# Last tile's products ahead of the first tiles' transposes, and one weights piece split by VectorE, in a two-layer decoder step

## The chip, the cores and the metric

The kernel runs on one core of a Trainium2 chip. The metric is the device time of one execution in microseconds. The core has five instruction streams: PE (TensorE: matrix products, transposes), DVE (VectorE), ACT (ScalarE), POOL (GpSimd) and SP, which here only issues transfers. Each runs its own instructions strictly in order and waits for the others on semaphores. An instruction that waits holds up everything behind it on its engine. Products land in PSUM, which has eight banks of 2 KB per partition; everything else lies in SBUF.

## The reference: what is computed

A two-layer decoder handles 512 prompt tokens and 8 x 4 = 32 sample tokens, 544 columns in all. Layer 0 mixes with a gated short convolution, layer 1 with multi-scale retention over four heads; each layer is followed by a SwiGLU feed-forward.

```python
x = x + mixer(rmsnorm(x))
x = x + (silu(h @ w_gate) * (h @ w_up)) @ w_down      # h = rmsnorm(x); 1024 -> 2816 -> 1024
```

Retention is computed in chunks. For each head and chunk it is

```python
scores = einsum(q, k) * decay
inner  = einsum(scores, v)
cross  = einsum(q, S) * cross_w
S_new  = S * chunk_decay + einsum(k * state_w, v)
```

and then `inner + cross` is normalised over the head's 512 columns (mean and variance), multiplied by `silu(g)` and a gain, and projected back. All is in float32.

## The kernel before

**Precision.** To keep float32 accuracy with the fast product type, each operand is split into a high half (rounded by ACT, `Copy` to fp32r) and a low half (the rest). Each product is then three: high by high, low by high, high by low. `split` (lines 182 to 184) lets ACT make the high half and DVE the low half by subtraction. `split_adding` (lines 186 to 190) spares DVE: ACT makes the high half and its negative, and a transfer issued by POOL adds the weights to that negative from memory. `load_piece` (line 131) loads one weights piece of 128 x 1024 by SP and takes the one or the other, by its argument `adding`. Weights buffers rotate through three slots.

**Feed-forward of a layer.** `whole_pairs` (line 524) does the first two rounds (m = 0 and 1) as plain products, four pieces each: gate for j = m and j = m + 11, then up for the same two (q = 0 and 1). Round 0's two gate pieces are interleaved by halves of k: first half of piece 0, first half of piece 1, second half of piece 0, second half of piece 1. All eight pieces of both layers come from `split_adding`. Ahead of that, the mixer's output projection adds its last tiles to x (L257), and `split_x` makes the halves of each tile of x (L194 on ACT, L195 on DVE), while POOL adds up squares (L210). The later rounds use a seven-product scheme with fewer products.

**Retention, per head.** After the values, gates and scores, the head works on four token tiles of 128 and on the sample rows:

- `inner(h, st, it)` (line 993) forms the products of one token tile into one PSUM bank: twelve for tiles 2 and 3.
- `sample_outputs(h, st, i)` (line 1046) multiplies the sample rows with the i-th quarter of the recurrent state S (four products, L1054, which the trace shows as eight), after S has been loaded by SP. S tiles rotate through three buffers, so the fourth (i = 3) is loaded once the first has been updated and written out.
- `states_update(h, st, i)` (line 1059) forms four products (L1070), adds them to the decayed S in two DVE steps (L1075) and writes S out (L1076).
- `normalized` (line 981) takes the statistics of a bank (L986, L987, L214 on DVE, the power -0.5 on POOL in L215) and writes the normalised tile to SBUF (L990). This frees the bank.
- `gated(h, st, yn, it)` (line 1010) transposes a normalised tile on PE (four transposes, L1014, into a bank) and multiplies the gate by it on DVE (L1017, or L1021 for the sample rows). This frees that bank.
- `qk_project(h + 1, ...)` (line 801) is the next head's key and query projection, 48 products of 272 columns each; given `inside`, it calls that between the two halves of k.

For heads 0 to 2 the next head's projections are interleaved with this head's last tiles (lines 1137 to 1158). Banks of this kind ("sm") are four: one collects the sample rows' outputs, the others are taken by tiles, transposes and the split projection, whichever is free in the order of the code. The order of instructions on each engine is then set by the framework's scheduler, by its own costs; `tc.issue_after` pins a start. In the order that was built before, the first two tiles' transposes have a bank each, and the last tile's products take the bank of the first.

Of the kernel before, what the change touches and what calls it, by code (L numbers as in the profile page):

```python
# [12 lines left out]
P = 128  # L13
D = 1024
KT = D // P
# [10 lines left out]
HJ = FJ // 2  # L26
# [19 lines left out]
def hybrid_decode_kernel(ctx: ExitStack, tc: tile.TileContext, a: dict, o: dict):  # L46
# [84 lines left out]
    def load_piece(src, n, parts=1, sw=None, keep=None, adding=False):  # L131

        if sw is None:
            w = wts.tile([P, n], F32, tag="w", name=nm("w"))
            wh, wl = parts2(n)
        else:
            w = sw.tile([P, n], F32, tag="w2", name=nm("w2"))
            wh, wl = parts2(n, sw, ("h2", "l2"))

        def load(i):  # L140
            c = slice(i * n // parts, (i + 1) * n // parts)
            last_load[0] = nc.sync.dma_start(w[:, c], src[:, c])
            if adding:
                split_adding(wh, wl, w, src)
            else:
                split(wh[:, c], wl[:, c], w[:, c])

        if keep is not None:
            keep.append(w)
        if parts > 1:  # L150
            return wh, wl, load
        load(0)
        return wh, wl
# [109 lines left out]
    with ExitStack() as c0:  # L263
# [7 lines left out]
        st = one.tile([P, KT, NB, 2], F32, tag="st", name="st")  # L271
# [221 lines left out]
    def ffn(layer, next_gain):  # L493
        with ExitStack() as c1:
            tp = c1.enter_context(tc.tile_pool(name=f"ff{layer}", bufs=4))
            fp = c1.enter_context(tc.tile_pool(name=f"ffp{layer}", bufs=2))
            sw = c1.enter_context(tc.tile_pool(name=f"sw{layer}", bufs=1))
# [26 lines left out]
            def whole_pairs():  # L524


                ks, us = list(range(KT)), []
                steps = rms_scale()
                for m in range(WHOLE):
                    gu, pts = [], []  # L530
                    ws = [
                        load_piece(a["ffgu"][layer, 2 * j + q], KT * P, sw=sw if m == 0 and q and j >= HJ else None, adding=True)
                        for q in range(2) for j in (m, m + HJ)
                    ]
                    for q in range(2):
                        pts.append([psum() for _ in range(2 - q)])
                        if m + q == 0:
                            for part in (ks[:KP], ks[KP:]):
                                for (wh, wl), pt in zip(ws, pts[0]):
                                    project(  # L540
                                        pt, wh, wl, 0, xh, xl, part[0] == ks[0], part[-1] == ks[-1], ks=part,
                                        weave=steps if part[0] else iter(()),
                                    )
                            continue
                        for i in range(2):
                            if i == len(pts[q]):
                                pts[q].append(psum())
                            project(pts[q][i], *ws[2 * q + i], 0, xh, xl, weave=steps)
                        drain(steps)
                    for q in range(2):  # L550
                        d = tp.tile([P, 2, T], F32, tag="gu", name=nm("gu"))
                        gu.append(d)
                        for i in range(2):
                            each(lambda p, di, r: nc.vector.tensor_mul(di, p, r), pts[q][i], halves(d[:, i, :]), R)
                            if q == 0:
                                nc.scalar.activation(d[:, i, :], d[:, i, :], AF.Silu)
                            else:
                                nc.vector.tensor_mul(d[:, i, :], d[:, i, :], gu[0][:, i, :])
                    us.append(gu[1])
                    for k in range(2 * m, KP if m == WHOLE - 1 else 2 * m + 2):  # L560
                        operand(k)
                return us
# [163 lines left out]
    with ExitStack() as c2:  # L726
# [74 lines left out]
        def qk_project(h, st, which, dt, inside=None):  # L801

            wh, wl = load_piece(a["rtqk"][h, which * 2 + dt], KT * P)
            pt = [bank(), bank()] if inside else psum()
            if inside:
                project(pt, wh, wl, 0, xh, xl, last=False, ks=range(KP))
                inside()
                project(pt, wh, wl, 0, xh, xl, first=False, ks=range(KP, KT))
            else:
                project(pt, wh, wl, 0, xh, xl)  # L810
            qk_rotate(st, which, dt, pt)
# [181 lines left out]
        def inner(h, st, it):  # L993

            vh, vl, _ = st["v"]
            qh, ql = st["q"]
            mh, ml = st["mid"]
            c = it // 2
            pt = bank()
            ts_ = token_tiles(it)  # L1000
            for dt in range(2 * c):
                mm3(pt, qh[:, dt, ts_], ql[:, dt, ts_], mh[:, dt, :], ml[:, dt, :], dt == 0, False)
            for jt in range(2 * c, it + 1):
                at = token_tiles((it % 2) if jt % 2 == 0 else 2)
                mm3(
                    pt, st["sh"][:, c, at], st["sl"][:, c, at], vh[:, jt, :], vl[:, jt, :], jt == 0, jt == it,
                )
            return pt
# [37 lines left out]
        def sample_outputs(h, st, i):  # L1046


            r, dt = RD[i]
            if i == 0:  # L1050
                st["po"] = bank()
                nc.tensor.matmul(st["po"], scp, st["vs"], start=True, stop=False, skip_group_check=True)
            for g in range(4):
                last_product[0] = nc.tensor.matmul(  # L1054
                    st["po"][32 * g : 32 * g + 8, :], qm[:, dt, g, r, :], st["S"][i][:, g, :],
                    start=False, stop=(i == 3), skip_group_check=True,
                )
# [51 lines left out]
        st = qk_start(0)  # L1109
        qk_first(st)  # L1110
        qk_project(0, st, 0, 1)
        for h in range(NH):
            more = h + 1 < NH
            value(h, st)
            st["S"] = {}
            for i in range(3):
                states_load(h, st, i)
            gate_project(h, st, 0)
            sample_operands(h, st)
            state(h, st, 0)  # L1120
            gate_project(h, st, 1)
            state(h, st, 1)
            for c in range(2):
                scores(h, st, c)
            if more:
                gate_project(h, st, 2)
                gate_project(h, st, 3)
            sample_outputs(h, st, 0)
            states_update(h, st, 0)
            states_load(h, st, 3)  # L1130
            yn0 = normalized(inner(h, st, 0))
            sample_outputs(h, st, 1)
            yn1 = normalized(inner(h, st, 1))
            states_update(h, st, 1)
            sample_outputs(h, st, 2)
            p2 = inner(h, st, 2)
            if more:
                nxt = qk_start(h + 1)
                for which in (1, 0):
                    qk_scale(nxt, which)  # L1140
                with tc.issue_after(last_product[0].ins):
                    qk_project(h + 1, nxt, 1, 0)
                with tc.issue_after(last_product[0].ins):
                    gated(h, st, yn0, 0)
                    gated(h, st, yn1, 1)
                yn2 = normalized(p2)
                sample_outputs(h, st, 3)
                p3 = inner(h, st, 3)
                yns = normalized(st["po"])
                states_update(h, st, 2)  # L1150
                gated(h, st, yn2, 2)
                yn3 = normalized(p3)
                qk_project(h + 1, nxt, 1, 1, lambda: states_update(h, st, 3))
                gated(h, st, yns, 4)
                gated(h, st, yn3, 3)
                qk_project(h + 1, nxt, 0, 0)
                qk_project(h + 1, nxt, 0, 1)
                out_project(h, st)
            else:
                yn2 = normalized(p2, "gt")  # L1160
                gate_project(h, st, 2, lambda: states_update(h, st, 2))
                sample_outputs(h, st, 3)
                yns = normalized(st["po"], "rot1")
                gate_project(h, st, 3, lambda: states_update(h, st, 3))
                for it, yn in enumerate((yn0, yn1, yn2)):
                    gated(h, st, yn, it)
                p3 = inner(h, st, 3)
                gated(h, st, yns, 4)
                yn3 = normalized(p3)
                out_project(h, st, [lambda: None, lambda: gated(h, st, yn3, 3)])  # L1170
            st = nxt
# [121 lines left out]
```

## Time and profile before

| | us |
|---|---|
| median of three runs | 1474.68 |
| lowest and highest | 1474.08, 1477.44 |
| the profiled execution | 1475.72 |
| its span | 1474.0 |
| PE busy | 1451.8 |
| DVE busy | 922.4 |
| ACT busy | 567.4 |
| POOL busy | 93.5 |

A row of the order of time gives the start and the length in microseconds from the span's start, the engine, the line of the kernel, the operation, "out <- in" by the program's names, the shape, and how many equal instructions it merges; in brackets stands how long the engine was idle before and what ended that. On PE, start to start is the better measure, since lengths overlap. A row of the list of waits gives the total, the number of times and the longest.

The last tiles of heads 0, 1 and 2, from the first tile's transposes to the next query projection, lie at 677.49 to 692.61, 804.10 to 818.76 and 930.23 to 944.88 us. Layer 1's feed-forward begins at 1084.27.

### The profile page before, as it was taken

Reading aid. Unit: us, or ns where it says so; the run is one execution under the profiler, and the core shown is the slowest. Engines: PE = TensorE matmul, PEld = TensorE weight load, DVE = VectorE, ACT = ScalarE, POOL = GpSimd, SP = SyncE. Lnnn points to the kernel's source line nnn. Section 1 sums busy time; section 2 is a strip of 40 time slices with the busy share of each in tenths; the row PEclk is TensorE's granted clock in tenths of the full one; section 3 lists DMA queues with packets and bytes.
Section 4 is the critical chain, followed back from the end, with each engine's and each line's share of the span. In section 5 each row is a group of like instructions: output and inputs, shape, how many; then the busy total and the mean of one; then the engine's idle time right before and its main releaser. Section 6 shows DMA issues by size and latency. Waiting matters only on the chain.

```text
span 1474.0 us, 25908 instructions
## 1 busy us (share of the span) xinstructions
PE 1451.8 (98%) x10954; PEld 1382.3 (94%) x10954; DVE 922.4 (63%) x1412; ACT 567.4 (38%) x805; POOL 93.5 (6%) x118
## 2 busy tenths in 40 slices
PE   8999999999999999999999999999999999999997
PEld 8999999999999999897987988888799999999996
DVE  5644439847748647648545834845849847748644
ACT  5222355625525434242142224214265625525333
POOL 2100220000000003000000000000030000000003
PEclk9999999999999999999999999999999999999998
DMA  5222264232322325336335613713474232322322
GB/s 210 87 93 94 89 169 108 96 103 88 103 95 87 101 65 190 106 115 233 98 115 171 201 58 117 267 34 139 172 171 116 92 106 90 94 94 91 98 66 81
DMA packets 69461, 173.36 MB, mean 118 GB/s; under 512 B 6480, under 2 KB 22992, under 8 KB 69344
## 3 DMA queue, kind: packets, MB, share of 16 engines
q1 hardware_dynamic: 66432, 162.12, 32.5%
q0 software_dynamic: 2336, 8.46, 3.4%
q8 instruction: 86, 1.41, 0.4%
q10 hardware_dynamic: 576, 1.11, 0.2%
q14 instruction: 31, 0.25, 0.1%
HBM read 150.50 MB, written 21.18 MB: 116 GB/s over the span
## 4 chain that ended last, share of the span: by engine, by line
PE 93%; DMA 4%; DVE 1%; ACT 1%; POOL 0%; issue 0%; SPq 0%; DVEq 0%; POOLq 0%; ACTq 0%
PE mm L170 41%; PE sm L427 26%; PE sm L170 14%; PE sm L848 2%; PE sm L849 2%; DMA S<-in_rets_dram 2%; PE sm L850 2%; PE sm L158 1%; PE sm L159 1%; PE sm L160 1%; DMA out_rets_dram<-S 1%; PE sm L1054 1%; PE mm L855 1%; DMA wl<-in_ffgu_dram 1%; DVE S L1075 0%; PE sm L1014 0%
## 5 line engine op out<-in xcount | busy, mean ns | idle before, releaser
L183 ACT ACTIVATE wh<-w 128x1024 fp32r<-128x1024 f32 (+2 forms) x211 | 208.4, 990 | 456.7 <-PE mm L170 271.8
L184 DVE TENSOR_TENSOR wl<-w,wh 128x1024 fp32r<-128x1024 f32 (+2 forms) x211 | 242.3, 1151 | 39.8 <-ACT wh L183 36.4
L170 PE MATMUL mm<-xh,wh 128*128 128x272 f32 x1060 | 221.7, 290 | 6.6 <-ACT wh L183 6.6
L170 PE MATMUL mm<-xh,wl 128*128 128x272 f32 x1060 | 219.6, 289 | 1.6 <-DMA wl<-in_ffgu_dram 1.6
L170 PE MATMUL mm<-xl,wh 128*128 128x272 f32 x1060 | 218.5, 288 | 0.0
L170 PEld LDWEIGHTS mm<-xh,wh 128*128 128x128 f32 x1060 | 166.4, 189 | 11.3 <-ACT wh L183 6.6
L170 PEld LDWEIGHTS mm<-xh,wl 128*128 128x128 f32 x1060 | 165.6, 189 | 2.2 <-DMA wl<-in_ffgu_dram 1.8
L427 PE MATMUL sm<-oh,wh 128*128 128x272 f32 x576 | 166.5, 289 | 0.0
L427 PE MATMUL sm<-oh,wl 128*128 128x272 f32 x576 | 166.5, 289 | 0.0
L170 PEld LDWEIGHTS mm<-xl,wh 128*128 128x128 f32 x1060 | 166.3, 189 | 0.0
L427 PE MATMUL sm<-ol,wh 128*128 128x272 f32 x576 | 166.2, 289 | 0.0
L257 DVE TENSOR_TENSOR x<-x,mm 128x544 f32<-128x544 f32 x85 | 61.2, 720 | 146.4 <-PE mm L170 146.4
L427 PE MATMUL sm<-oh,l 128*128 128x272 f32 x432 | 124.8, 289 | 0.0
L427 PE MATMUL sm<-ol,h 128*128 128x272 f32 x432 | 124.7, 289 | 0.0
L427 PE MATMUL sm<-oh,h 128*128 128x272 f32 x432 | 124.7, 289 | 0.0
L427 PEld LDWEIGHTS sm<-oh,wh 128*128 128x128 f32 x576 | 108.6, 189 | 0.4 <-ACT u L484 0.4
L427 PEld LDWEIGHTS sm<-oh,wl 128*128 128x128 f32 x576 | 108.7, 189 | 0.0
L427 PEld LDWEIGHTS sm<-ol,wh 128*128 128x128 f32 x576 | 108.5, 188 | 0.0
L184 DVE TENSOR_TENSOR l<-w,h 128x1024 fp32r<-128x1024 f32 x72 | 68.8, 956 | 55.2 <-ACT h L183 55.0
L170 PE MATMUL mm<-xh,f 128*128 128x272 f32 x576 | 99.3, 288 | 0.0
L210 POOL TENSOR_TENSOR sqacc<-sqacc,sq 128x544 f32<-128x544 f32 (+1 forms) x32 | 45.5, 1422 | 716.9 <-ACT sq L209 716.6
L170 PE MATMUL sm<-xh,wh 128*128 128x272 f32 x412 | 90.0, 293 | 0.5 <-DVE rs L214 0.3
(263 smaller groups left out, 2904.6 us busy)
## 6 DMA issues: line engine op xcount, KB each, us to landing
w<-in_ffgu_dram SPq DMA_DIRECT2D x88, 512.0 KB, 3.5
w<-in_ffdn_dram SPq DMA_DIRECT2D x96, 192.0 KB, 2.5
S<-in_rets_dram SPq DMA_DIRECT2D x16, 1024.0 KB, 7.3
out_rets_dram<-S SPq DMA_DIRECT2D x16, 1024.0 KB, 5.1
w<-in_cvin_dram SPq DMA_DIRECT2D x21, 512.0 KB, 3.5
w<-in_rtqk_dram SPq DMA_DIRECT2D x16, 512.0 KB, 3.6
w<-in_rtv_dram SPq DMA_DIRECT2D x16, 512.0 KB, 3.7
w<-in_rtg_dram SPq DMA_DIRECT2D x16, 512.0 KB, 4.1
```

Source lines behind the costliest of these rows:

```text
L158: nc.tensor.matmul(out, lh, rh, start=start, stop=False, skip_group_check=True)
L159: nc.tensor.matmul(out, lh, rl, start=False, stop=False, skip_group_check=True)
L160: last_product[0] = nc.tensor.matmul(out, ll, rh, start=False, stop=stop, skip_group_check=True)
L170: last_product[0] = nc.tensor.matmul(half(pt, hf)[:, :HT], w[:, c], act[k][:, hf * HT : (hf + 1) * HT], start=(first and k == ks[0] and i ...
L183: nc.scalar.activation(dh, src, AF.Copy)
L184: nc.vector.tensor_sub(dl, src, dh.bitcast(F32))
L210: nc.gpsimd.tensor_tensor(sqacc[:, c], sqacc[:, c], sq[:, c], op=ALU.add)
L257: last_residual[0] = nc.vector.tensor_add(xk, xk, p)
L427: nc.tensor.matmul(out, w[:, c], b[k][:, at, :], start=(first and k == 0 and i == 0), stop=(k == n - 1 and i == 2), skip_group_check=True,)
L848: nc.tensor.matmul(out, xh[kt][:, ts_], wh[:, cw], start=(kt == 0), stop=False)
L849: nc.tensor.matmul(out, xh[kt][:, ts_], wl[:, cw], start=False, stop=False)
L850: nc.tensor.matmul(out, xl[kt][:, ts_], wh[:, cw], start=False, stop=(kt == KT - 1))
```

## The change

In the heads with a successor, the last S quarter's outputs and the last token tile's products (`sample_outputs(h, st, 3)`, `inner(h, st, 3)`) are issued ahead of the first two tiles' transposes. The third tile's transposes move from ahead of the second key projection to between its halves of k, behind the last state update's products; the last tile's normalisation is issued after that projection. Head 3 is left as it was.

In the feed-forward, one of the sixteen whole pieces changes its split: layer 1, round 0, the gate piece for j = 11 (the second of the two that are interleaved) takes `split` in place of `split_adding`.

```diff
                     ws = [
-                        load_piece(a["ffgu"][layer, 2 * j + q], KT * P, sw=sw if m == 0 and q and j >= HJ else None, adding=True)
+                        load_piece(a["ffgu"][layer, 2 * j + q], KT * P, sw=sw if m == 0 and q and j >= HJ else None,
+                            adding=layer == 0 or m + q > 0 or j < HJ)
                         for q in range(2) for j in (m, m + HJ)
                     ]
@@
                 with tc.issue_after(last_product[0].ins):
                     qk_project(h + 1, nxt, 1, 0)
+                sample_outputs(h, st, 3)
+                p3 = inner(h, st, 3)
                 with tc.issue_after(last_product[0].ins):
                     gated(h, st, yn0, 0)
                     gated(h, st, yn1, 1)
                 yn2 = normalized(p2)
-                sample_outputs(h, st, 3)
-                p3 = inner(h, st, 3)
                 yns = normalized(st["po"])
                 states_update(h, st, 2)
-                gated(h, st, yn2, 2)
+
+                def inside():
+                    states_update(h, st, 3)
+                    gated(h, st, yn2, 2)
+
+                qk_project(h + 1, nxt, 1, 1, inside)
                 yn3 = normalized(p3)
-                qk_project(h + 1, nxt, 1, 1, lambda: states_update(h, st, 3))
                 gated(h, st, yns, 4)
                 gated(h, st, yn3, 3)
                 qk_project(h + 1, nxt, 0, 0)
```

Behind line 533 the changed kernel's lines are numbered one higher, and behind the reordered calls five.

## The prediction

> **What bounds the kernel now.** I read the page's first part, then the waits of TensorE (PE), then the order of time in the two places that the change touches.
>
> ```profile
> span 1474.0 us, 25908 instructions
> PE 1451.8 (98%) x10954; PEld 1382.3 (94%) x10954; DVE 922.4 (63%) x1412; ACT 567.4 (38%) x805; POOL 93.5 (6%) x118
> ```
>
> PE is busy for 98% of the span, so only what PE waits for can be won: 1474.0 - 1451.8 = 22 us, start and end included. The list of its waits says which of these the change can touch:
>
> ```profile
> PE mm L170 <- DMA wl<-in_ffgu_dram: 1.6, 1, 1.6
> PE sm L158 <- DVE gate L1017: 1.6, 3, 0.5
> PE sm L1054 <- DMA S<-in_rets_dram: 1.2, 4, 0.7
> ```
>
> The first is one stall in the second feed-forward. The other two lie in heads 0 to 2: three times half a microsecond before the last token tile's products (L158), and up to 0.7 us for the state S. All three together are 4.4 us, 0.3% of the span. The stretch of head 1 that is reordered, by engine:
>
> ```profile
> 804.10:818.76 14.66, 13.87 (x99) 10.87 (x97) 13.81 (x22) 1.85 (x2) 1.08 (x2) 1.00 0.60 209
> ```
>
> The columns after the length are PE, weight loads, DVE, ACT, POOL, granted clock (full), DMA share and GB/s. Here, unlike over the span, DVE (VectorE) is as busy as PE: 13.81 of 14.66 us. So the order of work on DVE counts as much as that on PE. PE in that stretch, in order of time:
>
> ```profile
> 804.10 1.03 PE L1014 MATMUL sm<-cb,yn 128*128 128x128 f32 x8
> 805.67 0.50 PE L158 MATMUL sm<-mid,qkh 128*128 128x512 f32 x1 [0.54 <-DVE gate L1017]
> 806.36 1.04 PE L1054 MATMUL sm<-S,qm 128*8 128x512 f32 x8 [0.19 <-DMA S<-in_rets_dram]
> 807.34 0.50 PE L159 MATMUL sm<-mid,qkh 128*128 128x512 f32 x1
> 809.75 0.39 PE L160 MATMUL sm<-vh,sl 128*128 128x512 f32 x1
> 810.07 0.51 PE L1070 MATMUL mm<-vs,kns 32*128 32x512 f32 x4
> 810.51 0.66 PE L1014 MATMUL sm<-cb,yn 128*128 128x128 f32 x4
> 810.92 0.37 PE L170 MATMUL sm<-xh,wh 128*128 128x272 f32 x1
> 814.42 0.50 PE L1070 MATMUL mm<-vs,kns 32*128 32x512 f32 x4
> 817.97 1.03 PE L1014 MATMUL sm<-cb,yn 128*128 128x128 f32 x8
> 818.76 0.50 PE L170 MATMUL mm<-xh,wh 128*128 128x272 f32 x2
> ...
> 677.49 1.03 PE L1014 MATMUL sm<-cb,yn 128*128 128x128 f32 x8
> 680.25 1.04 PE L1054 MATMUL sm<-S,qm 128*8 128x512 f32 x8 [0.68 <-DMA S<-in_rets_dram]
> ```
>
> Rows of several instructions give the start of the first. From start to start: a product of L158 to L160 takes about 0.235 us (ten steps from 807.34 to 809.75, the first 0.33), a transpose (L1014) 0.10, a pair of L170 0.25. And DVE with what it hands over, and one row of ACT (ScalarE):
>
> ```profile
> 804.30 0.72 DVE L816 TENSOR_TENSOR rot<-mm,gt 128x544 f32<-128x544 f32 x1 [3.96 <-PE mm L170]
> 804.94 1.28 DVE L1017 TENSOR_TENSOR gate<-gate,sm 128x512 f32<-128x512 f32 x2
> 806.13 0.81 DVE L990 TENSOR_SCALAR yn<-sm,mv,rs 128x512 f32<-128x512 f32 x1
> 807.48 0.70 DVE L986 BATCH_NORM_STATS2 bst<-sm 128x6 f32<-128x512 f32 x1 [0.53 <-PE sm L1054]
> 810.17 0.70 DVE L986 BATCH_NORM_STATS2 bst<-sm 128x6 f32<-128x512 f32 x1
> 811.51 2.34 DVE L1075 SCALAR_TENSOR_TENSOR S<-S,mm 128x1024 f32<-128x1024 f32 x2
> ...
> 804.05 1.06 ACT L183 ACTIVATE wh<-w 128x1024 fp32r<-128x1024 f32 x1 [12.34 <-PE mm L170]
> ...
> 1059.18 0.15 DVE L214 TENSOR_SCALAR rs<-mv 128x1 f32<-128x1 f32 x1
> 1060.11 0.81 DVE L990 TENSOR_SCALAR yn<-sm,mv,rs 128x512 f32<-128x512 f32 x1 [0.44 <-POOL rs L215]
> ```
>
> ```profile
> 1061.07 0.52 PE L1014 MATMUL sm<-cb,yn 128*128 128x128 f32 x3 [0.24 <-DVE yn L990]
> ```
>
> Handing over costs, from these rows: from the start of a gate multiplication (L1017) to the PE instruction that waits for it 805.67 - 804.94 = 0.73 us; from the start of a normalisation (L990) 1061.07 - 1060.11 = 0.96; from the start of the last product to its statistics (L986) 810.17 - 809.75 = 0.42; from rs (L214) over POOL to L990 0.93.
>
> **Part 1, the reordering in heads 0 to 2.** Nothing is added or removed; every product, transpose, DVE step and transfer keeps its size. In the built order PE now runs eight of the twelve products of the last tile, then the four pairs with S, the other four products, the first tile's transposes, the state products (L1070), the second tile's transposes, and the third tile's after the first product of the second half of k. DVE's order changes with it: the rotation's steps and the weights' split come ahead, then both statistics, and only then the first tile's multiplication.
>
> What is won first: the wait of L158 for the multiplication goes, since the tile's products now take a bank that is long free. But all of that lies ahead of S's arrival, and PE reaches S in 8 x 0.235 = 1.9 us, at 806.0, where S lands for 806.36; in head 0 at 677.49 + 1.9 = 679.4 against 680.25. S's load waits for an earlier state's write-out, which the change doesn't touch. So the pairs with S start at the same moment as before; call it T. At T seven products more are done (1.65 us) and eight transposes fewer (0.8 us): 0.85 us ahead.
>
> What comes then, by T = 806.36:
> - The S pairs take 0.98, four products 0.33 + 3 x 0.235 = 1.04: to T+2.0. Four transposes and four state products, 0.41 + 0.44 to 0.5: T+2.9.
> - The second tile's transposes write to the bank that the first tile's multiplication reads (they had a bank each before). That multiplication stands behind the last tile's statistics on DVE. The last product starts at T+1.78, statistics at +0.42 = T+2.20, 0.62 later (0.70 less overlap) the multiplication at T+2.82, and PE goes on at +0.73 = T+3.55. A stall of 0.6 us.
> - Transposes to T+3.96. The projection's bank is that of the third tile, freed by L990, which follows the multiplication by 0.60: T+3.42, and + 0.96 gives T+4.38. A stall of 0.4.
> - Before, the projection began at 810.92 = T+4.56, so it begins 0.2 earlier, but with the third tile's transposes (0.41) still to do. It loses less inside: before, 24 products took 3.50 us (810.92 to 814.42), 0.5 over 24 x 0.125, for a bank; now 3.0, to T+7.4. The second state's multiplications on DVE (two of 1.13, from T+4.9) end at T+7.3, just in time. State products 0.5, one product, and the third tile's transposes wait for the sample rows' L990 (starts T+7.2, + 0.96 = T+8.15; PE is there at T+8.1). Transposes 0.41, 23 products 2.9 and 0.1 for the change of kind: T+11.6. Before: 817.97 = T+11.61. Level.
> - Then four transposes and three products of the next projection: T+12.45. The last tile's L990 is now late: on DVE, T+7.9 after the sample rows, two state steps of 1.13, a multiplication 0.6, aggregation 0.1, rs at T+10.85, + 0.93 = T+11.8, and PE goes on at + 0.96 = T+12.75. A stall of 0.3. With the transposes done (0.4) and three products (0.375) taken off, the next projection stands where it would have begun at T+12.8; before it began at 818.76, T+12.40.
>
> So each head loses 0.4 us, three heads 1.2: the wait of 0.54 is replaced by one of 0.6 behind the statistics and one of 0.3 at the end. The bounds: the stretch without any wait behind T is about 11.1 us (0.98 + 1.04 + 0.41 + 0.5 + 0.41 + 6.0 + 0.5 + 0.5 + 0.8), so a head wins 1.3 at most; if every hand-over behind DVE comes 1 us later than summed, it loses 1.4. I take 0.4, since each hand-over has its own row.
>
> Queues that the steps pass: the third S's write-out (SP) follows the DVE step that ends at T+7.3, before 813.8 = T+7.4. The last S's comes 1 to 2 us earlier. The output weights' load, which waits for the split on DVE, is issued earlier, right behind the last S load's landing and beside loads for the next head, for which nothing waits. POOL's five small powers keep their order. All at nothing, covered by the 12 us of projection that follow; were that cover gone, the later last multiplication (0.8 us) would show.
>
> **Part 2, one weights piece in layer 1.** Piece 1 (gate, second half) loses ACT's L189 and POOL's adding transfer; DVE gets one L184.
>
> ```profile
> 1087.52 0.41 PE L170 MATMUL mm<-xl,wh 128*128 128x272 f32 x2
> 1089.51 0.51 PE L170 MATMUL mm<-xh,wl 128*128 128x272 f32 x2 [1.57 <-DMA wl<-in_ffgu_dram]
> 1089.86 0.41 PE L170 MATMUL mm<-xh,wh 128*128 128x272 f32 x2
> ...
> 1099.21 0.41 PE L170 MATMUL sm<-xh,wh 128*128 128x272 f32 x2
> ...
> 1078.23 1.06 ACT L188 ACTIVATE wh<-w 128x1024 fp32r<-128x1024 f32 x1 [0.26 <-PE sm L170]
> 1080.38 1.04 ACT L189 ACTIVATE wl<-wh 128x1024 fp32r<-128x1024 f32 x1
> ...
> 1068.44 1.22 DVE L184 TENSOR_TENSOR wl<-w,wh 128x1024 fp32r<-128x1024 f32 x1
> 1079.96 0.79 DVE L195 SCALAR_TENSOR_TENSOR xl<-x,vec,xh 128x544 fp32r<-128x544 f32 x1 [0.82 <-ACT xh L194]
> ...
> 1081.92 0.87 POOL L190 DMA_DIRECT2D wl<-in_ffgu_dram  x1
> 1087.78 0.88 POOL L190 DMA_DIRECT2D wl<-in_ffgu_dram  x1 [2.74 <-ACT wl L189]
> ...
> DMA to landing us min/median/max: 5.4/6.7/8.0
> ```
>
> Now the low half waits for L189, then POOL, then a transfer of 7.5 us (1081.92 to 1089.5). After: high half at 1079.3, L184 in a DVE gap of 0.82, done by 1080.6, against a need at 1087.8. It pushes L195 back by 0.5; its tile belongs to the second half of k, which PE reaches after 1089.86. The stall goes whole: PE would have taken this pair at 1087.52 + 0.25 = 1087.77, and the pair costs 0.35 (to 1089.86) instead of 0.25: 1.74 + 0.1 = 1.84 us. Next in line is piece 2, from POOL at 1087.78: landing at 1095.8 at the longest, needed by the third pair of that piece, at 1099.71 - 1.84 = 1097.9. Piece 1's weights buffer is freed 1.3 us later, for a piece of the next round. I take -1.8; the bounds are -1.8 and 0.
>
> A transfer of this kind is priced by the Trainium skill, "DMA: Bandwidth & Descriptors", Anatomy of one DMA, at about 2.0 us plus the bytes at 436 GB/s, which makes 3.2 us for 512 KB (estimate). By it the piece would have landed at 1085.1, nothing would be won here, and the sum would be +1.2 in place of -0.6. The trace disagrees, with 5.4 to 8.0 us for the transfers of this line and the stall itself, and the measurement decides.
>
> **Sum.** 3 x 0.4 - 1.8 = -0.6 us. The profiled execution took 1475.72 us, 1.0 above the median of 1474.68; taken from the median it gives 1474.1 us. The three runs lie 0.23% apart, so a change under 0.2% (2.9 us) can't be told from none.
>
> **Rivals.**
> - The reordering wins (faster, 1469.0): the waits behind DVE overlap with PE's pipeline and each head wins its bound, 1474.68 - 3 x 1.3 - 1.8. For it: two banks' waits do disappear. Against: DVE at 13.81 of 14.66 us has no room, and the stall comes from its order. It decides from 0.4 won per head.
> - The chain behind the statistics is longer (slower, 1477.7): any lateness of DVE at the first multiplication now passes through three PE waits one to one. With 1.2 us more per head, 3 x 1.6 - 1.8 = +3.0. For it: DVE has 0.85 us free in the stretch, and a split of 1.2 now stands ahead. Against: that split's turn comes at 804.30 + 0.64 + 0.64 = 805.6 and its input from ACT is there at 805.1. It decides from 1.2 us.
> - The stall of part 2 moves on, so that the change does not do what it says there (no change, 1475.9): piece 2 or DVE's L195 is late instead. Against: 2.1 us of room at the longest transfer of the trace.
>
> **How the numbers follow.** My forecast 0.58, the moved stall 0.12 (both within 0.2%: 0.70), the winning order 0.16, the longer chain 0.14. The range takes in the moved stall, the longer chain and a part of the way to the winning order: 1471.0 to 1478.0 us. The likeliest case by itself is 1473 to 1475.5.
>
> **What would show it.** Right: L1054 starts in heads 0 to 2 as before; the second tile's transposes wait for the multiplication (L1018 after the change) some 0.6 us, L170 for L991, the last transposes for L991; from T to the next projection 12.8 us less its three products; no wait of L170 for in_ffgu. Wrong: no wait of transposes for the multiplication, an L1054 that starts earlier, or a new wait for wl between the first stall's place and the end of that feed-forward's first pieces.

## The result and the profile after

| | before | after |
|---|---|---|
| median, us | 1474.93 | 1477.45 |
| lowest and highest, us | 1473.2, 1477.44 | 1475.78, 1478.86 |
| executions | 20 | 20 |
| the profiled execution, its span, us | 1475.72, 1474.0 | 1477.7, 1475.9 |

The ratio is 1.0015, with a 95% interval of 1.0009 to 1.0022: the change costs about 2.2 us (1.3 to 3.2), where 0.6 us were forecast to be won. The time lies in the forecast's range; its sign is the other. The change is under the 0.2% that the forecast, from three executions, took as the least that can be told from none; with twenty of each kernel it is told, by little.

The page of the changed kernel, its first lines:

```profile
span 1475.9 us, 25893 instructions
PE 1452.4 (98%) x10954; PEld 1382.7 (94%) x10954; DVE 924.7 (63%) x1413; ACT 566.8 (38%) x804; POOL 93.4 (6%) x117
```

The work is nearly the same (PE 0.6 us more, one instruction from ACT to DVE, one transfer fewer on POOL), so the difference lies in waits. PE's, from its list of waits (total, number, longest):

```profile
PE sm L1055 <- DMA S<-in_rets_dram: 1.6, 3, 0.7
PE sm L1015 <- DVE gate L1018: 1.5, 3, 0.5
PE sm L1015 <- DVE yn L991: 1.4, 4, 0.4
PE mm L878 <- DVE v L874: 0.8, 1, 0.8
PE sm L170 <- DVE yn L991: 0.5, 3, 0.2
```

As forecast, the wait of L158 for a gate and the wait for `in_ffgu` are gone, and the transposes (L1015) and L170 wait in their place. Not forecast is L878, one wait of 0.84 us in `value` of head 1, code that the change does not touch. PE in the reordered stretch of head 1, in order of time:

```profile
808.59 1.05 PE L1055 MATMUL sm<-S,qm 128*8 128x512 f32 x8 [0.49 <-DMA S<-in_rets_dram]
810.60 0.60 PE L1015 MATMUL sm<-cb,yn 128*128 128x128 f32 x4
812.14 0.66 PE L1015 MATMUL sm<-cb,yn 128*128 128x128 f32 x4 [0.51 <-DVE gate L1018]
812.95 0.36 PE L170 MATMUL sm<-xh,wh 128*128 128x272 f32 x1 [0.15 <-DVE yn L991]
816.13 0.51 PE L1071 MATMUL mm<-vs,kns 32*128 32x512 f32 x4
820.13 0.60 PE L1015 MATMUL sm<-cb,yn 128*128 128x128 f32 x4
821.49 0.66 PE L1015 MATMUL sm<-cb,yn 128*128 128x128 f32 x4 [0.38 <-DVE yn L991]
```

With T = 808.59, the second tile's transposes start at T+3.55, the projection at T+4.36, its second half's state products at T+7.54, the sample rows' transposes at T+11.54 and the last tile's at T+12.90. The last ones are held by DVE, which itself waits for POOL:

```profile
820.62 0.81 DVE L991 TENSOR_SCALAR yn<-sm,mv,rs 128x512 f32<-128x512 f32 x1 [0.72 <-POOL rs L215]
```

To compare kernels I use four lengths on PE, from start to start. They are read from the order of time of each kernel and shown in a table behind the experiments: from the fourth S quarter's products (T) to the next head's first value product (L856 here, L855 before); from there to L878 in head 1; from the third to the fourth S quarter's products; and from head 3's fourth S quarter to PE's last row, a stretch that holds the second feed-forward.

### The profile page after: what moved, and what is told of

Same layout as the page of the kernel before. It is cut to its first block, busy times and chain, and to the rows that moved or that the text cites. A ratio compares the mean times of both kernels' runs of the same rounds, so it can differ in the third digit from the quotient of the medians.

```text
span 1475.9 us, 25893 instructions
## 1 busy us (share of the span) xinstructions
PE 1452.4 (98%) x10954; PEld 1382.7 (94%) x10954; DVE 924.7 (63%) x1413; ACT 566.8 (38%) x804; POOL 93.4 (6%) x117
## 4 chain that ended last, share of the span: by engine, by line
PE 93%; DMA 3%; DVE 3%; ACT 0%; POOL 0%; issue 0%; SPq 0%; DVEq 0%; POOLq 0%; ACTq 0%
PE mm L170 41%; PE sm L427 26%; PE sm L170 13%; PE sm L849 2%; PE sm L850 2%; PE sm L851 2%; DMA S<-in_rets_dram 2%; DMA out_rets_dram<-S 1%; PE sm L158 1%; PE sm L160 1%; PE sm L159 1%; DVE S L1076 1%; PE sm L1055 1%; PE mm L856 1%; DVE yn L991 0%; DVE wl L184 0%
## 5 line engine op out<-in xcount | busy, mean ns | idle before, releaser
L184 DVE TENSOR_TENSOR wl<-w,wh 128x1024 fp32r<-128x1024 f32 (+2 forms) x212 | 243.5, 1152 | 42.5 <-ACT wh L183 37.4
L170 PE MATMUL mm<-xh,wh 128*128 128x272 f32 x1060 | 222.0, 291 | 6.8 <-ACT wh L183 6.8
L170 PE MATMUL mm<-xh,wl 128*128 128x272 f32 x1060 | 219.7, 289 | 0.0
L170 PE MATMUL mm<-xl,wh 128*128 128x272 f32 x1060 | 219.5, 288 | 0.0
L170 PEld LDWEIGHTS mm<-xh,wh 128*128 128x128 f32 x1060 | 166.6, 189 | 11.5 <-ACT wh L183 6.8
L170 PEld LDWEIGHTS mm<-xl,wh 128*128 128x128 f32 x1060 | 166.8, 189 | 0.0
L170 PEld LDWEIGHTS mm<-xh,wl 128*128 128x128 f32 x1060 | 165.9, 189 | 0.4
L184 DVE TENSOR_TENSOR l<-w,h 128x1024 fp32r<-128x1024 f32 x72 | 68.8, 956 | 54.7 <-ACT h L183 54.2
L170 PE MATMUL mm<-xh,f 128*128 128x272 f32 x576 | 99.2, 288 | 0.0
L170 PE MATMUL sm<-xh,wh 128*128 128x272 f32 x412 | 90.5, 293 | 0.7 <-DVE yn L991 0.5
```

Of the source, the lines that this page charges most:

```text
L170: last_product[0] = nc.tensor.matmul(half(pt, hf)[:, :HT], w[:, c], act[k][:, hf * HT : (hf + 1) * HT], start=(first and k == ks[0] and i ...
L184: nc.vector.tensor_sub(dl, src, dh.bitcast(F32))
```

## The experiments

**The changed kernel again, and each part alone.** The first runs ask which part costs what, and whether the wait at L878 was one execution's chance. No edit:

> The changed kernel once more, unchanged. Theory A (the loss is in the kernel): 1476 to 1479 us, and in the new profile the gate weights' split in head 1 (ScalarE, L183) is late again and TensorE waits about 0.8 us at L878 behind it, and the S pairs of head 3 are 0.5 us later than after head 2's end again. Theory B (these two are one execution's chance, a transfer that landed 1.3 us later than in the profile before): the time is the same, but the wait at L878 is not there, and the pair's shifts between the S pairs' starts (+0.4, +0.25, +0.15) come out otherwise. In both the last tile's part of each head, from the S pairs' start to the next head's start, is again 0.4 to 0.6 us longer than before.

Measured: 1.0013 (1.0004 to 1.0021), 1475.93 against 1474.46 us. T to the next head is 60.23 to 60.26 us in all three heads, as in the first profile. The wait at L878 is there again, but shorter:

```profile
758.03 0.65 PE L878 MATMUL mm<-v,sum 128*32 128x512 f32 x2 [0.57 <-DVE v L874]
```

The S pairs of head 3, which were 0.5 us late in the first profile, are not late here (11.14 us behind the third pairs, before 11.15). So the wait at L878 belongs to the changed kernel, and head 3's lateness was chance.

The feed-forward edit alone (only the `adding=` line of the diff):

> The kernel before with the feed-forward edit alone (the low part of one piece of weights made by VectorE). As forecast, and as the pair of traces shows it: 1.8 us faster than before (1473.1), no wait of TensorE for that low part in the second feed-forward. Rival: the 1.8 us that the trace gains there are given back behind it, and the time is within 0.5 us of before.

Measured: 1.0000 (0.9991 to 1.0008), 1474.07 against 1474.46 us. There is no wait for the low part in its trace, and still next to nothing is won: the interval (at most 1.3 us won) leaves out the 1.8 us of the forecast.

The reordering alone (all of the diff but that line):

> The kernel before with the reordering of the heads alone. Theory A (the feed-forward edit's 1.8 us hold and the heads cost what the median says): 2.2 + 1.8 = 4.0 us slower than before. Theory B (the heads cost only what the last tile's part shows, three times 0.55 us, and the rest of the profile's shift is chance): 1.7 us slower. The forecast on record had 1.2 us slower.

Measured: 1.0011 (1.0002 to 1.0020), 1475.72 against 1474.46 us, 1.3 by the medians and 1.6 by the ratio. That is theory B's number, and the interval (0.3 to 2.9 us) leaves out theory A's. It is not all of theory B, though: the wait in head 1 is in this trace again (0.83 us). The kernel still splits the piece by a transfer, and its trace waits 1.27 us for it, 0.3 less than the profile before.

Half of the reordering:

```diff
                 with tc.issue_after(last_product[0].ins):
                     qk_project(h + 1, nxt, 1, 0)
+                sample_outputs(h, st, 3)
+                p3 = inner(h, st, 3)
                 with tc.issue_after(last_product[0].ins):
                     gated(h, st, yn0, 0)
                     gated(h, st, yn1, 1)
                 yn2 = normalized(p2)
-                sample_outputs(h, st, 3)
-                p3 = inner(h, st, 3)
                 yns = normalized(st["po"])
```

> The kernel before with half of the reordering: the last tile's products and its S pairs are issued ahead of the first two tiles' transposes, while the third tile's transposes stay ahead of the second projection. Theory 1 (the first tile's multiplication, put behind the last tile's statistics on VectorE, is the costly half): the loss of the whole reordering is here too, 0.4 to 0.6 us a head, 1.2 to 1.8 us in all, and more by up to 0.4 us a head, since the third tile's transposes then wait for their own rows ahead of the projection. Theory 2 (the cost is in the third tile's transposes between the halves of k and the last tile's behind the projection): within 0.5 us of before.

Measured: 1.0009 (1.0000 to 1.0018). From T to the next head it takes 59.96 us, 0.25 more than before, where the whole reordering takes 0.55 more. So neither theory holds as written: this half costs a little under half. It has the same stall of the second tile's transposes:

```profile
811.20 1.38 PE L1014 MATMUL sm<-cb,yn 128*128 128x128 f32 x8 [0.51 <-DVE gate L1017]
```

**Undoing one wait each.** First tile ahead of the last tile's products, the rest as in the changed kernel:

```diff
+                with tc.issue_after(last_product[0].ins):
+                    gated(h, st, yn0, 0)
                 sample_outputs(h, st, 3)
                 p3 = inner(h, st, 3)
                 with tc.issue_after(last_product[0].ins):
-                    gated(h, st, yn0, 0)
                     gated(h, st, yn1, 1)
```

> The changed kernel with the first tile's transposes and multiplication back ahead of the last tile's products; the second tile's stay behind them. If the 0.5 us stall of the second tile's transposes (they wait for the first tile's multiplication, which stood behind the last tile's statistics on VectorE) is what the first half of the reordering costs: no such stall, and from the S pairs' start to the next head's start 0.3 to 0.5 us less in each of three heads than in the changed kernel, 0.9 to 1.5 us in all, less whatever the wait of head 1 does. Rival (the stall is moved on to the next wait, that of the projection for the third tile's normalized rows): no more than 0.1 us a head.

Measured: 0.9986 (0.9977 to 0.9995), 1472.50 against 1474.25 us. T to the next head is 59.1 us, 1.14 less than in the changed kernel and 0.6 less than before. PE in head 1, in order of time, T = 805.37:

```profile
803.22 0.60 PE L1015 MATMUL sm<-cb,yn 128*128 128x128 f32 x4
805.37 1.04 PE L1055 MATMUL sm<-S,qm 128*8 128x512 f32 x8
807.85 0.60 PE L1015 MATMUL sm<-cb,yn 128*128 128x128 f32 x4
808.81 0.39 PE L170 MATMUL sm<-xh,wh 128*128 128x272 f32 x1
816.61 0.60 PE L1015 MATMUL sm<-cb,yn 128*128 128x128 f32 x4
819.18 0.60 PE L1015 MATMUL sm<-cb,yn 128*128 128x128 f32 x4
```

No row has a bracket: the three waits of the changed kernel are gone together. DVE in the changed kernel, then here:

```profile
810.80 0.70 DVE L987 BATCH_NORM_STATS2 bst<-sm 128x6 f32<-128x512 f32 x1 [0.40 <-PE sm L160]
811.41 0.67 DVE L1018 TENSOR_TENSOR gate<-gate,sm 128x512 f32<-128x512 f32 x1
812.00 0.81 DVE L991 TENSOR_SCALAR yn<-sm,mv,rs 128x512 f32<-128x512 f32 x1
```

```profile
804.06 0.68 DVE L1018 TENSOR_TENSOR gate<-gate,sm 128x512 f32<-128x512 f32 x1
804.66 0.81 DVE L991 TENSOR_SCALAR yn<-sm,mv,rs 128x512 f32<-128x512 f32 x1
```

The first tile's multiplication is over before the statistics come, so the third tile's normalisation starts at T-0.71 instead of T+3.41, and the projection begins at T+3.44 instead of T+4.36. That ends the first two waits, and more is won than the 0.3 to 0.5 us a head that were expected. The third wait may have ended for another reason. The scheduler built more of the order anew: seventeen products, not three, now stand between the sample rows' transposes and the last ones (T+11.24 and T+13.81), and DVE's split of the weights (L184) starts at T+7.01 instead of T-0.91. So the run prices this order as a whole, and what the early multiplication is worth by itself is not shown.

The last tile's normalisation ahead of the projection again:

```diff
+                yn3 = normalized(p3)
                 qk_project(h + 1, nxt, 1, 1, inside)
-                yn3 = normalized(p3)
```

> The changed kernel with the last tile's normalization ahead of the projection again, so that only the third tile's transposes lie between the halves of k. If the last transposes' wait (0.38 us a head for their own rows, VectorE L991) is a cost by itself: that wait is gone, 0.2 to 0.4 us a head less than in the changed kernel. Rival: VectorE then does that work in front of what the projection's tiles wait for, the wait turns up ahead of the projection (as in the kernel with the first half alone, where it was 0.15 us), and the time is within 0.3 us of the changed kernel.

Measured: 0.9997 (0.9989 to 1.0006), 1473.71 against 1474.25 us. T to the next head is 59.67, 0.58 less than in the changed kernel and level with before. The last transposes start 0.57 behind the sample rows' and wait for nothing:

```profile
817.56 0.60 PE L1015 MATMUL sm<-cb,yn 128*128 128x128 f32 x4
818.13 0.60 PE L1015 MATMUL sm<-cb,yn 128*128 128x128 f32 x4
```

The wait's bracket said 0.38 us; taking it away wins 0.58 from start to start. A bracket counts from the modelled end of the product ahead, 0.29 us behind its start, while products that wait for nothing follow one another every 0.125 us. The rival is wrong, for the wait ahead of the projection keeps its size:

```profile
810.38 0.36 PE L170 MATMUL sm<-xh,wh 128*128 128x272 f32 x1 [0.16 <-DVE yn L991]
```

In the heads this kernel differs from the first half alone only by the third tile's transposes between the halves of k, and it takes 0.29 us less (59.67 against 59.96). So that move wins, and what the second half of the reordering loses is the late normalisation.

**Head 1's wait.** In the trace PE waits at L878 for DVE, DVE for ACT, and ACT for a gate weights' piece. ACT's row before and after:

```profile
753.01 1.06 ACT L183 ACTIVATE wh<-w 128x1024 fp32r<-128x1024 f32 x1
```

```profile
755.30 1.06 ACT L183 ACTIVATE wh<-w 128x1024 fp32r<-128x1024 f32 x1 [1.30 <-DMA w<-in_rtg_dram]
```

Behind that row on ACT stand the values' own splits and L873, for which DVE and PE wait. SP issues the piece at the same place, 9.07 us behind the start of the value products (749.01 and 749.97), and no other transfer is under way. Before, it lands in 3.9 us; after, in 5.2. The list of transfers, by queue, from 10.0 to 13.0 us behind that start, before and after:

```profile
q1 hardware_dynamic: 144, 0.52, 54.3%
```

```profile
q1 hardware_dynamic: 141, 0.52, 48.6%
q8 instruction: 1, 0.02, 2.0%
```

A 16 KB packet of an instruction queue has come in between. That queue moves 86 such packets in every kernel here, and PE's stream has 22,014 recorded instructions before (2 x 10,954 matrix instructions and weight loads, and waits): one packet for 256 of them. Counted in all fourteen traces, this packet, the 45th, starts when PE has begun 151 to 179 instructions more than 44 x 256. The changed kernel has 22,005, nine waits fewer, three a head; with fewer instructions ahead of it, the same packet comes later in the work: 10.08, 10.72 and 12.16 us behind that start in three executions of the changed kernel, 9.75 and 9.83 in two of the kernel before. Only head 0's three of the nine lie ahead of this place. Three instructions are some 0.35 us here (a product and its weight load take 0.235), as in the earliest of the three (10.08 against 9.75); why the others are later still is not known. The test leaves the order alone and puts twelve small products at the start. The trace shows them as 24 products and 24 weight loads, so later instructions stand 48 places further on, not the 24 of the expectation:

```diff
     last_product = [None]
+    ahead = [12]
...
         ks = list(ks or range(len(ah)))
+        while ahead[0]:
+            ahead[0] -= 1
+            nc.tensor.matmul(half(pt, 0)[:, :16], ones, ones[:, :16], start=True, stop=True)
         for k in ks:
```

> The changed kernel with twelve small matmuls (128x16, of constants, into a bank that the first projection overwrites) put at its very start, where TensorE waits 6.6 us for the first weights anyway: nothing else is moved, but every later instruction of TensorE stands some 24 places further on in its stream. Theory F (the wait of head 1 at L878 comes from a 16,384-byte packet of TensorE's instruction queue, which comes every 256 of its instructions and in the reordered kernels falls into the transfer of a gate weights' piece): the packet, at 10.1 to 12.3 us behind the start of head 1's value matmuls (L856) in the reordered kernels, comes 1 to 3 us earlier, ahead of that transfer (10.0 to 12.6); the piece lands in 3.9 us instead of 5.0 to 5.2, TensorE does not wait at L878, and the time is 0.6 to 1.0 us under that of the changed kernel. Theory G (the new order of the heads' work delays that piece itself): the wait of 0.6 to 1.0 us is still there and the time is the changed kernel's.

Measured in the trace: the packet now lies 7.75 us behind the start of head 1's value products (748.05 to 751.05 us in the list of transfers: that packet alone, and the piece issued there, landing in 3.6 us), and the stretch to L878 is 17.74 us, as before the change:

```profile
q8 instruction: 1, 0.02, 2.6%
issues: line engine op xcount, KB each, median us to landing
w<-in_rtg_dram SPq DMA_DIRECT2D x1, 512.0 KB, 3.6
...
758.79 0.63 PE L882 MATMUL mm<-v,sum 128*32 128x512 f32 x2
```

(L882 is this kernel's number for L878.) Theory F holds for the wait, in one trace. The time does not bear it out and does not settle its price: 1.0014 (1.0005 to 1.0023), where the changed kernel had 1.0013 and 1.0015 beside other runs of before, and the intervals are wider than the 0.5 to 1.0 us in question.

**The feed-forward edit.** Why does the edit win nothing, though its stall is gone? It was run a second time:

> The feed-forward edit alone, a second time, to narrow its interval. If the stall that it takes away is as long in most executions as in the profile before (1.6 us, 1.8 with what follows it): 1.4 to 1.8 us faster than before. If that profile was a long case (the reordered kernels without the edit showed 1.3 and 0.4 us): 0.4 to 1.0 us faster.

Measured: 1.0001 (0.9992 to 1.0010), 1474.30 against 1474.25 us: nothing won, less than either expectation. The interval (at most 1.2 us won) leaves out the first and not the second. Then the kernel before, for another trace, with no edit:

> The kernel before, unchanged, for one more trace of the feed-forward stall (1.57 us of wait in the trace before, 1.27 and 0.43 in two others without the edit) and of the places that the change did not touch (the start-up and the S pairs' waits). If the stall is mostly under 1 us, so is it here; head 1's value matmuls do not wait at L877.

It took 1473.99 us in its one execution, and has no wait for the low part at all. The rows at the place of the stall, without a bracket:

```profile
1087.63 0.41 PE L170 MATMUL mm<-xl,wh 128*128 128x272 f32 x2
1087.88 0.41 PE L170 MATMUL mm<-xh,wl 128*128 128x272 f32 x2
```

The product with the low part (wl) follows a quarter of a microsecond behind the one ahead of it. The transfer that POOL issues for that low part, in five traces of kernels without the edit, in the order before, this one, the reordering alone, its first half, and the kernel of the next paragraph:

```profile
wl<-in_ffgu_dram POOLq DMA_DIRECT2D x1, 512.0 KB, 7.5
```

```profile
wl<-in_ffgu_dram POOLq DMA_DIRECT2D x1, 512.0 KB, 5.5
```

```profile
wl<-in_ffgu_dram POOLq DMA_DIRECT2D x1, 512.0 KB, 7.2
```

```profile
wl<-in_ffgu_dram POOLq DMA_DIRECT2D x1, 512.0 KB, 6.4
```

```profile
wl<-in_ffgu_dram POOLq DMA_DIRECT2D x1, 512.0 KB, 6.9
```

All are issued 35.6 us behind head 3's last S pairs and land after 5.5 to 7.5 us; PE waits 1.57, 0, 1.27, 0.43 and 0.89 us. One microsecond of landing is one of stall, beyond about 6 us. The stall was real, and the profile before had the longest of five.

Last, the kernel with the first tile ahead, without and with the edit, on one chip:

> The kernel with the first tile's multiplication kept ahead of the last tile's products, without the feed-forward edit. It stands against the same kernel with the edit, on the same chip: if the edit saves what the traces of kernels without it show (1.84, 1.56 and 0.80 us of delay between the last S pairs and the span's end, mean 1.4), this one is 1.4 us slower than that one, and its trace waits for the low part at the second feed-forward; if most executions have a shorter wait than those three traces, 0.2 to 0.6 us slower; and 0 if the edit costs elsewhere what it saves there.

> The same kernel with the feed-forward edit, a second time: 1.0 to 2.2 us faster than before (1.75 the first time), from the S pairs' start to the next head's start 59.1 us again (59.7 before, 60.25 in the changed kernel).

Measured: without the edit 1473.65 us, 0.9992 (0.9983 to 1.0001); with it 1472.93, 0.9992 (0.9983 to 1.0001); before 1474.04. The medians are 0.7 us apart, the ratios not at all. So over three pairs the edit wins between nothing and 0.7 us by the medians and nothing by the ratios, with intervals some 2.5 us wide. That it costs elsewhere what it saves is not what the traces show: with it, head 3's last S pairs lie 417.7 to 417.8 us ahead of PE's last row, and 417.77 in the trace of the kernel before that had no stall; the code ahead of them is the same. And the kernel with the first tile ahead is the fastest of the study, 1.75 and 1.1 us under before in its two sets, though only the first interval excludes no change. The changed kernel, beside them:

> The changed kernel a third time, on the chip of the kernels beside it: 1.5 to 2.2 us slower than before; from the S pairs' start to the next head's start 60.25 us; a wait at L878 in head 1 of 0.6 to 1.0 us.

Measured: 1.0015 (1.0006 to 1.0023), 1476.25 against 1474.04 us. The wait at L878 comes a third time, 0.35 us by its bracket, less than the 0.6 to 1.0 expected.

The lengths (us), from the starts of the rows; "T to next" is the mean of heads 0 to 2, which agree within 0.05, "S" the mean from the third to the fourth S pairs in those heads:

| kernel | T to next | value products to L878, head 1 | S | last S pairs to the end |
|---|---|---|---|---|
| before; once more | 59.71; 59.69 | 17.74; 17.79 | 11.58; 11.36 | 419.58; 417.77 |
| after; again; third | 60.26; 60.25; 60.27 | 18.74; 18.47; 18.26 | 11.49; 11.29; 11.42 | 417.75; 417.73; 417.75 |
| reordering alone | 60.25 | 18.74 | 11.75 | 419.30 |
| its first half | 59.96 | 18.24 | 11.35 | 418.53 |
| feed-forward edit alone, twice | 59.73; 59.71 | 17.75; 17.88 | 11.43; 11.35 | 417.75; 417.75 |
| more PE instructions | 60.25 | 17.74 | 11.43 | 417.73 |
| last normalisation early | 59.67 | 17.74 | 11.37 | 417.74 |
| first tile ahead, twice | 59.11; 59.12 | 17.75; 18.17 | 11.58; 11.54 | 417.78; 417.78 |
| the same without the edit | 59.11 | 18.04 | 11.43 | 418.97 |

## Why the prediction was wrong, step by step

- **T does not move: right.** The S pairs came on average 11.29 to 11.49 us behind the third ones in the changed kernel, 11.36 and 11.58 before. Single heads (0 to 2) of all kernels lie between 11.1 and 12.3 us, and no trend shows. (Of the four waits for S that the prediction puts in these heads, one, of 0.19 us, is head 3's; nothing hangs on it.)
- **Behind T: right in each wait, short by 0.15 us in the end.** Forecast and measured: second tile's transposes T+3.55 and T+3.55, projection T+4.38 and T+4.36, sample rows' transposes T+11.6 and T+11.54, last transposes T+12.75 and T+12.90. The mis-sized term is the last stall, taken as 0.3 us. The last normalisation starts at T+12.03, where T+11.8 was summed, and putting it back wins 0.58 a head. So a head loses 0.55 where 0.4 was forecast, and three lose 1.65 instead of 1.2.
- **"All at nothing" for the queues: right for those named, but one was not named.** PE's own instruction queue is also passed. In three traces of the changed kernel head 1's value products take 1.00, 0.73 and 0.52 us more, 0.75 on average. The reordering did not add to that work; by the traces a shifted instruction packet held up its weights.
- **"The stall goes whole ... I take -1.8": this is the step that failed.** The stall does go whole, in every trace with the edit (417.7 to 417.8 us behind the last S pairs). But its 1.84 us were the price of one execution. Over five traces without the edit it was 1.83, 0.02, 1.55, 0.78 and 1.22 (the table's last column less 417.75), mean 1.1, and the two medians with the edit alone say 0.4 won and 0.05 lost. The prediction itself showed transfers of this line landing after 5.4 to 8.0 us and took 7.5 for all executions; it also took the end of its own bounds (-1.8 to 0). At the median of those transfers, 6.7 us, the stall is some 0.8 us shorter, and the sum would have had the other sign: 1.2 - 1.0. With the stall at 1.84 us, the heads' greater loss alone would not have turned it (1.65 - 1.84).
- **The sum.** 1.65 + 0.75 - (0 to 1.1) = 1.3 to 2.4 us, against 2.2, 1.9 and 2.2 measured. The 0.75 is from traces alone: the kernel whose trace lacks it was no faster (2.1 us behind before, by its ratio), and without it the sum is 0.6 to 1.7. That the sum meets the time is therefore no proof of its terms. The rival "chain behind the statistics is longer" had the time (1477.7) but not the cause: it wanted 1.2 us more a head, and a head lost 0.15 more.
- **"The reordering wins"** was priced from waits that overlap. They did not. Another order does win: with the first tile kept ahead, the waits go and a head wins 0.6 us.

What stays open: why the adding transfer lands after 5.5 us or after 7.5 when it is issued at the same place, why the instruction packet's place varies between executions of one kernel, what it costs in the median, and why the edit's medians show less than the 1.1 us of the traces.

## What to carry to other kernels

A wait for a transfer that a profile shows once is one draw: before pricing its removal, look at the spread of landing times of the same kind of transfer and price the middle, or take a second profile. When a row of small waits hangs on one late engine, ask what made it late first; here, keeping one tile's transposes and multiplication ahead of two statistics gave an order without the three waits, while the reordering as a whole lost. A wait in code that was not touched may still be the change's, if the number of instructions ahead of it changed.

## What was not expected of the hardware

An instruction packet and a weights' transfer got in each other's way. In fourteen traces the start of that packet behind head 1's value products goes with the delay at L878. At 9.75 to 9.94 us, just ahead of the weights' packets (from 10.0), the delay is 0 to 0.14 us; at 10.08 to 10.72, 0.30 to 0.73; at 12.16 and 12.31, at the end of the transfer, 1.00 both times; at 7.75, none. The Trainium skill, "Runtime: NRT & Kernel Launch", Instruction fetch mechanics, says that an engine refills its instructions in blocks of 16 KiB, 256 instructions, over its own DMA queue, and that this is mostly hidden. The traces agree with the size and the rate (86 packets of 16 KB for 22,014 instructions of PE). PE itself shows no delay beside a packet that meets no such transfer (at 7.75 us the stretch to L878 is 17.74 us, as before). But a 512 KB transfer of data landed up to 1.3 us later beside such a packet, and that reached PE.
